# One change at six places of an encoder kernel: order of loads, more tiles, and where the low-rank products and the output projection stand

## The chip, the cores and the metric

The kernel runs on one core of a Trainium2 chip. Its time is the device time of one execution, in microseconds (us). Before the change the median of three runs is 2454.44 us (2453.6 to 2456.31). The engines are TensorE (PE: matmuls; PEld is its loading of the stationary operand), VectorE (DVE), ScalarE (ACT), GpSimd (POOL) and SyncE (SP). Transfers between the chip's memory and a core are issued by SP and by ACT, each in the order of its own instruction stream.

## The reference

An encoder trunk of two layers works on 1024 tokens of width 1024, in float32. Each layer normalizes, mixes tokens, adds to the residual stream, normalizes again, and runs a SwiGLU feed-forward network (FFN) of hidden width 2816 (22 blocks of 128), again added to the residual stream. Cut to the parts that matter here:

```python
for layer in range(2):
    hn = rms_norm(h, mix_norm[layer])
    if layer % 2 == 0:
        h = h + hybrid_ab_mixer(hn, ...)        # spatial gating and pooling
    else:
        y, v_first = rwkv7_time_mix(hn, ...)    # recurrence over time
        h = h + y
    hn = rms_norm(h, ffn_norm[layer])
    h = h + (silu(hn @ w_gate) * (hn @ w_up)) @ w_down
return rms_norm(h, final_norm)
```

The time mixing of layer 1 makes `r`, `k`, `v` by full products, the decay and learning rate by low-rank products (`tanh(xw @ w1) @ w2`, `(xa @ a1) @ a2`), the gate by `sigmoid(xg @ g1) @ g2`. Then a state of 64x64 per head is carried over the 1024 tokens, the result is normalized per head, multiplied by the gate and sent through `w_o`.

## The kernel before, in words

The sequence is cut into two halves of 512 tokens (`h` = 0 and 1; `HT` = 512). Activations lie transposed, as 8 blocks of 128 features by 512 tokens (`KT` = 8). To keep float32 accuracy every operand is split in a high and a low part (`whi`, `wlo`; `ahi`, `alo`: `split`, a copy on ACT and a subtraction on DVE, L157 and L158). A product of one 128x128 block of weights takes three matmuls of 128x512 (`mm3`, L399 to L401). A dense block of 128 outputs is 24 matmuls.

A plan (`push`) lists all weights in the order in which they are used. `take` splits the next weight of the plan, and issues on ACT the load of the one or two behind it, into one of three `raw` tiles; the splits go to `whl()` (three tiles each of `whi` and `wlo`, L125) unless the plan names another place. Each output is summed in a bank of PSUM. In the stages of the FFN there are five such banks (`DENSE`, L390), beside the recurrence three. `residual` (L493) adds a bank to the residual stream `H[h]` on DVE and so frees it.

Work that would leave PE idle runs beside dense work: `drive` and `beside` advance one generator by the progress of another. Final instruction order on each engine comes from a scheduler that follows priorities and a simulated timeline, so the rows of order below are what the engines really get. An engine works its own rows strictly in that order.

The six places, in order of time:

1. **Down products of layer 0, half 0** (L1876 to L1900). The hidden blocks of layer 0 were made earlier and saved in memory (`hid_d`, L743). `down_steps` (L883) takes groups of two and three hidden blocks in turn, loads each block on SP (L894) into one of the tiles `hd`, or of the tiles that an earlier stage lent (`lw`, `lh`: rows that read `ahi<-hid_d`), multiplies with the down weights (`dhi`, `dlo`) and adds to `H[0]`. The residual stream of half 0 comes back by L1890 (blocks 4 to 7; the first four blocks of the first group use the lent tiles, L914), that of half 1 by L1896.
2. **The first down groups of half 1** (L1881, L1907). Four groups of three run beside the normalization and the gate of layer 1's time mixing. `project_norm` (L1088) writes the normalized activations `hn`, then `project_gate` mixes and splits them. `ahead=False` lets a group's loads wait until it begins; `slots_of(f, 4, 3)` gives four weight tiles and three activation tiles.
3. **The second product of the gate** (`project`, L1207 to L1214): eight outputs, each copied by ACT (L1212) into one of four tiles (two names, two tiles each) and stored on SP.
4. **The recurrence** (`recur`, L1440 on). `load(c)` (L1472) loads a chunk of 64 tokens on SP: `ar`, `bk` (the keys; one tile), `uv`, `XT`. At the first chunk the norm weights `lnw` (L1620) follow, and `post` loads the gate chunk `gch` and the value chunk `vch` (L1640, L1642). The state passes from half 0 to half 1 in an SBUF tile, `state_d`.
5. **Beside half 1's gate** (L1975). The eight output weights of half 0 and the first FFN blocks run beside the mixing of half 1; `LOWRANK_AT[1] = 8` puts the low-rank first products (48 matmuls with splits) after the eighth output weight, `GATE_AT[1] = 8` the gate's (48) behind them. `norm_a`, the norm of half 0 ahead of the FFN, starts there too.
6. **End of layer 1** (L2001 to L2004). The FFN of half 0 goes on with blocks 18 and 19, then half 1's output projection, then its norm, then blocks 20 and 21 of half 0 and the whole FFN of half 1. In `ffn` with `early`, gate and up products run ahead of the down product of an earlier group as `ffn_events` lists them.

Of the kernel before, what the change touches and what calls it, by code (L numbers as in the profile page):

```python
# [28 lines left out]
LOWRANK_AT, GATE_AT, MIX_AT = (2, 8), (3, 8), (1, 2)  # L29
# [14 lines left out]
def tile_trunk(  # L44
# [309 lines left out]
    push_ffn(1, 0, G1A[2], push_act(("y", 1), y_d[1]))  # L354
    for e in push_o(1):
        e()
    push_ffn(1, 0, G1A[3])
# [525 lines left out]
    def down_steps(h, groups, wslot, hslot, ahead=True, after=None, between=iter(()), at={}, first={}):  # L883

        held = {}
# [4 lines left out]
        def load(g):  # L890
            for f in g:
                if f not in held:
                    held[f] = hslot(f)
                    sp.dma_start(held[f].bitcast(F32), hid_d[h][:, f])  # L894
# [5 lines left out]
        def steps():  # L900
            for gi, g in enumerate(groups):
                load(g)
                wd = {f: take(("d", 0, h, f)) for f in g}
                if gi in at:
                    at[gi]()
                if ahead and gi + 1 < len(groups):
                    load(groups[gi + 1])
# [25 lines left out]
    def ffn(l, h, hn, fp, groups=GROUPS, last=False, nd=3, after=None, between=iter(()), early=False):  # L933
# [3 lines left out]
        for kind, f in ffn_events(groups, early):  # L937
# [25 lines left out]
            elif kind == "t":  # L963
                wd[f] = take(("d", l, h, f))
            else:
                for ff in f:
                    if not early:
                        wd[ff] = take(("d", l, h, ff))
                if last and f == groups[-1]:
                    yield from final_down(h, f, wd, hid, turned)  # L970
                    continue
                for m in range(KT):
                    o = mmt()
                    ms = slice(m * P, (m + 1) * P)
                    for i, ff in enumerate(f):
                        mm3(o, wd[ff][0][:, ms], wd[ff][1][:, ms], *hid[ff], i == 0, i == len(f) - 1)
                    residual(m, h, o)
                    if after is not None and f == groups[-1]:
                        after(m)
                    yield len(f) / 8  # L980

# [202 lines left out]
    def project(h, hn1, kp, ring, keep, before_v):  # L1184
# [21 lines left out]
        for m in range(KT):  # L1206
# [4 lines left out]
            t = tmp(("epx", "k")[m % 2], 2)  # L1211
# [225 lines left out]
    state_d = const.tile([P, 8, 64], F32, name="state_d")  # L1437
    pool.memset(state_d, 0.0)

    def recur(h, wp, stream):  # L1440
# [12 lines left out]
        C, ypair, loaded = {}, {}, [None]  # L1453
        S, Q, last = [state_d], {}, []
# [18 lines left out]
        def load(c):  # L1473
# [3 lines left out]
            sp.dma_start(bk, bk_d[h][c])  # L1477
# [83 lines left out]
        def burst(c, bkt, w1):  # L1561
# [32 lines left out]
            if cg < NCH - 1:  # L1594
                Sn = state_d if c == 7 else wt("S", 2, [P, 8, 64])
# [5 lines left out]
                S[0] = Sn  # L1601
                yield 0.1
# [8 lines left out]
            if more:  # L1611
# [5 lines left out]
                if c == 0:  # L1617
                    with tc.issue_after(loaded[0].ins):
# [79 lines left out]
        load(0)  # L1698
        with tc.issue_after(loaded[0].ins):
# [170 lines left out]
    for e in (wp_es, f_es, xt_es, actp_es, ps_es):  # L1870
# [8 lines left out]
    wslot, hslot = slots_of(f, 4, 3)  # L1879
    odd = {g: i % 2 for i, gs in enumerate(D0A) for g in gs}  # L1880
    prime_b, steps_b = down_steps(1, D0B[0], wslot, hslot, False, lambda m: sp.dma_start(h_d[1, 0][:, m, :], H[1][:, m, :]))  # L1881
    acc, add = running_sums(0)
    prime_a, steps_a = down_steps(
        0, D0A, lambda f: (lw, wslot)[odd[f]](f), lambda f: (lh, hslot)[odd[f]](f), after=add, at={len(D0A) - 1: prime_b}, first=first,
# [4 lines left out]
    for k in range(4, KT, 2):  # L1889
        a_loaded = sp.dma_start(H[0][:, k : k + 2, :], hm_d[0][:, k : k + 2, :])  # L1890

    def wa1():
        yield 2.0
        for k in range(0, KT, 2):
            with tc.issue_after(a_loaded.ins):
# [105 lines left out]
    drive(ffn(1, 0, hnA, f, G1A[2], between=take_act(("y", 1)), early=True))  # L2001
    exhaust(out_proj(1, ys))
    hnB = norm_split(1, C_FFN + 8, b)
    drive(ffn(1, 0, hnA, f, G1A[3], last=True, early=True))  # L2004
# [33 lines left out]
```

## Time and profile before

| | value |
|---|---|
| runs, median (lowest to highest) | 2454.44 us (2453.6 to 2456.31) |
| span of the profiled execution | 2450.8 us, 3.6 us under that median |
| PE busy | 97% of the span, 15567 matmuls |
| DVE busy | 60% |
| ACT busy | 38% |
| POOL busy | 9% |
| PE's longest wait | 9.7 us, for `hd<-hid_d` |
| memory traffic | 342.17 MB, mean 140 GB/s |

A row of the waits names the engine that waits, the tile that it writes and the line, then what released it: another engine or a transfer (DMA) with its tile and line, and the total, the number and the longest of these waits. A timeline's row has its start and length in us from the start of the span. In brackets stands the idle time of the engine before it, and what ended that. SPq and ACTq rows are issues of transfers; the transfer itself lands later. Matmul rows overlap: a row's 0.39 us is its length from entry to exit, while the distance from one start to the next is what each one costs. The column PEclk is the clock granted to TensorE, 1.00 being full.

### The profile page before, as it was taken

How to read it: one execution, taken by the hardware profiler on the slowest of the kernel's cores; microseconds unless marked ns; L12 is line 12 of the kernel's file. 1: busy time of each engine (PE TensorE's matmuls, PEld its weight loads, DVE VectorE, ACT ScalarE, POOL GpSimd, SP SyncE). 2: the span in 40 equal slices, each digit the busy share in tenths (PEclk: the TensorE clock that was granted, in tenths of full speed). 3: DMA queues.
4: the chain of work that ended last, by engine and by line, in shares of the span. 5: the costliest groups of instructions: out<-in, count | busy, mean ns of one | idle time of the engine just before them, and what ended most of it. 6: DMA issues, size and time to landing. Idle time of an engine off the chain costs nothing. (4 is left out here: it accounts for less than half of the span.)

```text
span 2450.8 us, 38190 instructions
## 1 busy us (share of the span) xinstructions
PE 2369.0 (97%) x15567; PEld 1945.9 (79%) x15567; DVE 1476.8 (60%) x2328; ACT 935.9 (38%) x1403; POOL 217.1 (9%) x246
## 2 busy tenths in 40 slices
PE   8999999999899999999999999999999999999998
PEld 6888888888687788778777678777888788888887
DVE  6445766655558758856767947856664446434443
ACT  6233444443114644422335744433232324322223
POOL 0200000000000033101100133201100001000001
PEclk9999999999999999999999999999999999999999
DMA  5114443334655554774435465675433422433231
GB/s 177 52 60 140 153 146 103 113 103 155 252 203 204 165 149 131 226 212 132 129 126 155 160 166 141 186 223 158 143 112 122 129 78 90 150 105 95 86 103 52
DMA packets 406767, 342.17 MB, mean 140 GB/s; under 512 B 78080, under 2 KB 351616, under 8 KB 405824
## 3 DMA queue, kind: packets, MB, share of 16 engines
q10 hardware_dynamic: 266048, 195.33, 26.3%
q1 hardware_dynamic: 140544, 144.41, 18.8%
q8 instruction: 122, 2.00, 0.3%
q14 instruction: 53, 0.43, 0.0%
HBM read 263.07 MB, written 76.61 MB: 139 GB/s over the span
## 5 line engine op out<-in xcount | busy, mean ns | idle before, releaser
L399 PE MATMUL mm<-ahi,whi 128*128 128x512 f32 x1376 | 541.0, 394 | 5.8 <-DVE h L493 3.7
L400 PE MATMUL mm<-alo,whi 128*128 128x512 f32 x1376 | 541.5, 394 | 1.1 <-DVE alo L158 1.1
L401 PE MATMUL mm<-ahi,wlo 128*128 128x512 f32 x1376 | 540.1, 393 | 1.4 <-DVE wlo L158 1.4
L157 ACT ACTIVATE whi<-raw 128x1024 fp32r<-128x1024 f32 (+1 forms) x280 | 282.0, 1013 | 557.4 <-PE mm L400 428.6
L158 DVE TENSOR_TENSOR wlo<-raw,whi 128x1024 fp32r<-128x1024 f32 (+1 forms) x280 | 328.4, 1177 | 246.5 <-ACT whi L157 231.0
L399 PEld LDWEIGHTS mm<-ahi,whi 128*128 128x128 f32 x1376 | 259.0, 188 | 63.1 <-ACT whi L157 6.2
L401 PEld LDWEIGHTS mm<-ahi,wlo 128*128 128x128 f32 x1376 | 259.2, 188 | 58.4 <-DVE wlo L158 2.7
L400 PEld LDWEIGHTS mm<-alo,whi 128*128 128x128 f32 x1376 | 259.3, 188 | 57.7 <-issue 2.5
L493 DVE TENSOR_TENSOR h<-h,mm 128x512 f32<-128x512 f32 x276 | 185.5, 684 | 162.5 <-PE mm L401 161.6
L399 PE MATMUL mm<-hidhi,wdhi 128*128 128x512 f32 x304 | 117.5, 395 | 2.9 <-ACT hidhi L958 2.3
L400 PE MATMUL mm<-hidlo,wdhi 128*128 128x512 f32 x304 | 119.7, 394 | 0.0
L401 PE MATMUL mm<-hidhi,wdlo 128*128 128x512 f32 x304 | 119.0, 391 | 0.0
L730 PE MATMUL mm<-ahi,whi 128*128 128x512 f32 x296 | 115.6, 390 | 0.0
L731 PE MATMUL mm<-alo,whi 128*128 128x512 f32 x296 | 115.2, 389 | 0.0
L732 PE MATMUL mm<-ahi,wlo 128*128 128x512 f32 x296 | 113.6, 389 | 0.0
L157 ACT ACTIVATE wdhi<-raw 128x1024 fp32r<-128x1024 f32 x42 | 43.5, 1058 | 168.0 <-PE mm L400 133.1
L955 DVE TENSOR_TENSOR sg<-sg,mm 128x512 f32<-128x512 f32 x52 | 35.7, 687 | 118.9 <-PE mm L401 118.7
L399 PE MATMUL mm<-hd,dhi 128*128 128x512 f32 x192 | 75.8, 396 | 13.8 <-DMA hd<-hid_d 10.8
L400 PE MATMUL mm<-hd,dhi 128*128 128x512 f32 x192 | 75.9, 395 | 0.0
L401 PE MATMUL mm<-hd,dlo 128*128 128x512 f32 x192 | 74.8, 393 | 0.0
L399 PEld LDWEIGHTS mm<-hidhi,wdhi 128*128 128x128 f32 x304 | 57.3, 189 | 16.0 <-ACT hidhi L958 2.7
L401 PEld LDWEIGHTS mm<-hidhi,wdlo 128*128 128x128 f32 x304 | 57.5, 189 | 11.9
(395 smaller groups left out, 4278.2 us busy)
## 6 DMA issues: line engine op xcount, KB each, us to landing
raw<-in_ffn_w_down_dram ACTq DMA_DIRECT2D x88, 512.0 KB
raw<-in_ffn_w_gate_dram ACTq DMA_DIRECT2D x74, 512.0 KB
raw<-in_ffn_w_up_dram ACTq DMA_DIRECT2D x74, 512.0 KB
hid_d<-hid SPq DMA_DIRECT2D x36, 512.0 KB
hd<-hid_d SPq DMA_DIRECT2D x26, 512.0 KB
raw<-in_ab_w_in_dram ACTq DMA_DIRECT2D x16, 512.0 KB
raw<-in_ab_w_out_dram ACTq DMA_DIRECT2D x16, 512.0 KB
raw<-in_rwkv_w_r_dram ACTq DMA_DIRECT2D x16, 512.0 KB
```

What stands on the lines that cost most here:

```text
L157: act.activation(hi, src, AF.Copy)
L158: (eng or dve).tensor_tensor(out=lo, in0=src, in1=hi.bitcast(F32), op=ALU.subtract)
L399: pe.matmul(o, whi, xhi, start=first, stop=False)
L400: pe.matmul(o, whi, xlo, start=False, stop=False)
L401: pe.matmul(o, wlo, xhi, start=False, stop=last)
L493: dve.tensor_tensor(out=H[h][:, m, :], in0=H[h][:, m, :], in1=o, op=ALU.add)
L730: pe.matmul(o, wh[:, k, :], x[0][:, k, :], start=st, stop=False, skip_group_check=True)
L731: pe.matmul(o, wh[:, k, :], x[1][:, k, :], start=False, stop=False, skip_group_check=True)
L732: pe.matmul(o, wl[:, k, :], x[0][:, k, :], start=False, stop=k == 3, skip_group_check=True)
L955: dve.tensor_tensor(out=s, in0=s, in1=o, op=ALU.mult)
```

## The change

All edits keep what is computed.

- Place 1: the loads of the second group's activations come first; then `H[0]`'s blocks 4 to 7, which now wait in SP's order behind the last load of activations issued so far (`rest_a`, called when the first group starts); then the next groups' loads and `H[1]` in turn.
- Place 2: four activation tiles, not three; the next group's loads are issued one group ahead; the third weight of each group goes to the tiles of `whl()` that the side weights use, so that the four weight tiles hold two weights of two groups. In `down_steps` the next group's load now also stands ahead of the call `at[gi]`.
- Place 3: the copies use four names with two tiles each, eight in all.
- Place 4: `lnw` waits for the issue of the keys of chunk 2 as well, and `gch` and `vch` stand behind `lnw` as before. The state is stored to memory after half 0 and loaded at half 1.
- Place 5: the low-rank first products and their weights stand two output weights earlier.
- Place 6: blocks 18 to 21 are one call of `ffn`. The gate of block 20 now runs before the down product of 18 and 19; the output projection and the norm of half 1 are called after that down product (`then`). The plan of weights follows.

SP's transfers at place 1, before (tile written, tile read, size, count; `hid_d_77` is half 0, `hid_d_78` half 1, `hm_d` the saved residual streams):

```order
L743 DMA hid_d_77<-hid 128x1024
L743 DMA hid_d_78<-hid 128x1024
L1890 DMA h<-hm_d_75 128x1024 x2
L1896 DMA h<-hm_d_76 128x1024 x4
L894 DMA hd<-hid_d_77 128x1024 x3
L894 DMA ahi<-hid_d_77 128x1024
L894 DMA alo<-hid_d_77 128x1024
```

The same place in the changed kernel:

```order
L747 DMA hid_d_77<-hid 128x1024
L747 DMA hid_d_78<-hid 128x1024
L898 DMA hd<-hid_d_77 128x1024 x3
L1900 DMA h<-hm_d_75 128x1024 x2
L898 DMA hd<-hid_d_77 128x1024
L898 DMA ahi<-hid_d_77 128x1024
L898 DMA alo<-hid_d_77 128x1024
L1913 DMA h<-hm_d_76 128x1024 x2
L898 DMA hd<-hid_d_77 128x1024 x2
L1913 DMA h<-hm_d_76 128x1024 x2
```

The three activation loads moved ahead of all six loads of the residual streams, and half 1's stream moved behind the third group's activations.

DVE at place 2, before, from the norm's last step over the eight scalings to the second group's residuals (`hn_5521` is the normalized tile):

```order
L443 TENSOR_TENSOR ndg<-ident,nrs 128x512
L493 TENSOR_TENSOR h<-h,mm 128x512 x3
L158 TENSOR_TENSOR dlo<-raw,dhi 128x1024
L1088 SCALAR_TENSOR_TENSOR hn_5521<-h,vec,aux 128x512 x8
L493 TENSOR_TENSOR h<-h,mm 128x512
L158 TENSOR_TENSOR dlo<-raw,dhi 128x1024 x2
L158 TENSOR_TENSOR alo<-hn_5521,ahi 128x513
L1171 SCALAR_TENSOR_TENSOR mix<-hn_5521,vec,mix 128x512
L158 TENSOR_TENSOR alo<-hn_5521,ahi 128x513
L1171 SCALAR_TENSOR_TENSOR mix<-hn_5521,vec,mix 128x512
L158 TENSOR_TENSOR alo<-hn_5521,ahi 128x513 x6
L493 TENSOR_TENSOR h<-h,mm 128x512 x3
```

In the changed kernel:

```order
L447 TENSOR_TENSOR ndg<-ident,nrs 128x512
L497 TENSOR_TENSOR h<-h,mm 128x512 x2
L158 TENSOR_TENSOR dlo<-raw,dhi 128x1024
L497 TENSOR_TENSOR h<-h,mm 128x512
L158 TENSOR_TENSOR dlo<-raw,dhi 128x1024
L158 TENSOR_TENSOR wlo<-raw,whi 128x1024
L1094 SCALAR_TENSOR_TENSOR hn_5520<-h,vec,aux 128x512 x8
L158 TENSOR_TENSOR alo<-hn_5520,ahi 128x513 x2
L1177 SCALAR_TENSOR_TENSOR mix<-hn_5520,vec,mix 128x512 x2
L497 TENSOR_TENSOR h<-h,mm 128x512
L158 TENSOR_TENSOR alo<-hn_5520,ahi 128x513
L497 TENSOR_TENSOR h<-h,mm 128x512
```

The second group's weights are now split ahead of the eight scalings, no residual of the first group is left behind them, and the second group's residuals alternate with the splits of the activations.

SP at place 4, half 0, before:

```order
L1475 DMA ar<-ar_d_1974 128x1024
L1490 DMA XT<-xi_d_1984 32x8x32
L1620 DMA lnw<-in_rwkv_ln_w_dram 64x8x64 x2
L1640 DMA gch<-g_d_1982 128x8x128
L1642 DMA vch<-v_d_1978 64x2x512 x2
L1480 DMA uv<-v_d_1978 64x512
L1481 DMA uv<-v_d_1978 64x512
L1477 DMA bk<-bk_d_1976 128x1024
```

In the changed kernel:

```order
L1482 DMA ar<-ar_d_1974 128x1024
L1497 DMA XT<-xi_d_1984 32x8x32
L1487 DMA uv<-v_d_1978 64x512
L1488 DMA uv<-v_d_1978 64x512
L1484 DMA bk<-bk_d_1976 128x1024
L1629 DMA lnw<-in_rwkv_ln_w_dram 64x8x64 x2
L1649 DMA gch<-g_d_1982 128x8x128
L1651 DMA vch<-v_d_1978 64x2x512 x2
```

The keys of chunk 2 and the two loads ahead of them passed the five loads for the output norm.

The diff, cut:

```diff
...
 RATIO, AHEAD, INV, FINE = 3.0, 450, 5, 1
-LOWRANK_AT, GATE_AT, MIX_AT = (2, 8), (3, 8), (1, 2)
+LOWRANK_AT, GATE_AT, MIX_AT = (2, 6), (3, 8), (1, 2)
...
     push_ffn(1, 0, G1A[1])
-    push_ffn(1, 0, G1A[2], push_act(("y", 1), y_d[1]))
-    for e in push_o(1):
-        e()
-    push_ffn(1, 0, G1A[3])
+    y1, o1 = push_act(("y", 1), y_d[1]), push_o(1)
+    for i, e in enumerate(e for e in ffn_events(G1A[2] + G1A[3], True) if e[0] != "d"):
+        if e == ("u", G1A[3][0][0]):
+            for go in o1:
+                go()
+        push_ffn_event(1, 0, *e)
+        if e[0] in "gu":
+            next(y1, None)
     push_ffn(1, 1)
...
-    def down_steps(h, groups, wslot, hslot, ahead=True, after=None, between=iter(()), at={}, first={}):
-
-        held = {}
+    def down_steps(h, groups, wslot, hslot, ahead=True, after=None, between=iter(()), at={}, first={}, loaded=None):
+
+        held, loaded = {}, [] if loaded is None else loaded
         for g in groups:
...
                     held[f] = hslot(f)
-                    sp.dma_start(held[f].bitcast(F32), hid_d[h][:, f])
+                    loaded.append(sp.dma_start(held[f].bitcast(F32), hid_d[h][:, f]).ins)
...
                 wd = {f: take(("d", 0, h, f)) for f in g}
+                if ahead and gi + 1 < len(groups):
+                    load(groups[gi + 1])
                 if gi in at:
                     at[gi]()
-                if ahead and gi + 1 < len(groups):
-                    load(groups[gi + 1])
                 for m in range(KT):
...
-    def ffn(l, h, hn, fp, groups=GROUPS, last=False, nd=3, after=None, between=iter(()), early=False):
+    def ffn(l, h, hn, fp, groups=GROUPS, last=False, nd=3, after=None, between=iter(()), early=False, then={}):
         dests["d"] = lambda: (fp.tile([P, D], F32R, tag="wdhi", bufs=nd, name="wdhi"),
...
                     yield len(f) / 8
+                if f[-1] in then:
+                    then[f[-1]]()
...
             pe.matmul(o, g2b[:96, ms], keep["gst"][:96], start=False, stop=True)
-            t = tmp(("epx", "k")[m % 2], 2)
+            t = tmp(("k", "epx", "av", "sg")[m % 4], 2)
             act.activation(t, o, AF.Copy)
...
             )
-    state_d = const.tile([P, 8, 64], F32, name="state_d")
-    pool.memset(state_d, 0.0)
+    state_d = dram.tile([P, 8, 64], F32, name="state_d")
...
         lnw = wt("lnw", 1, [P, 8, 64])
-        C, ypair, loaded = {}, {}, [None]
-        S, Q, last = [state_d], {}, []
+        C, ypair, loaded, keys = {}, {}, [None], [None]
+        S, Q, last = [wt("S", 2, [P, 8, 64])], {}, []
+        if h == 0:
+            pool.memset(S[0], 0.0)
...
             bk = wt("bk", 1, [P, 8, 2, 64])
-            sp.dma_start(bk, bk_d[h][c])
+            keys[0] = sp.dma_start(bk, bk_d[h][c])
             uv = wt("uv", 2, [P, 2, 8, 64])
...
             if cg < NCH - 1:
-                Sn = state_d if c == 7 else wt("S", 2, [P, 8, 64])
+                Sn = wt("S", 2, [P, 8, 64])
                 os_ = smt()
...
                 S[0] = Sn
+                if c == 7:
+                    sp.dma_start(state_d, Sn)
                 yield 0.1
...
                 if c == 0:
-                    with tc.issue_after(loaded[0].ins):
+                    with tc.issue_after(loaded[0].ins), tc.issue_after(keys[0].ins):
                         for r in range(2):
...
         load(0)
+        if h:
+            sp.dma_start(S[0], state_d)
         with tc.issue_after(loaded[0].ins):
...
     ha_pool, ha_es = open_pool(name="ha0", bufs=1, side="left")
-    wslot, hslot = slots_of(f, 4, 3)
+    wslot, hslot = slots_of(f, 4, 4)
     odd = {g: i % 2 for i, gs in enumerate(D0A) for g in gs}
-    prime_b, steps_b = down_steps(1, D0B[0], wslot, hslot, False, lambda m: sp.dma_start(h_d[1, 0][:, m, :], H[1][:, m, :]))
+    third = {g[2] for g in D0B[0]}
+    prime_b, steps_b = down_steps(1, D0B[0], lambda f: whl() if f in third else wslot(f), hslot, True, lambda m: sp.dma_start(h_d[1, 0][:, m, :], H[1][:, m, :]))
     acc, add = running_sums(0)
+    hid_loads = []
+
+    def rest_a():
+        for k in range(4, KT, 2):
+            with tc.issue_after(hid_loads[-1]):
+                sp.dma_start(H[0][:, k : k + 2, :], hm_d[0][:, k : k + 2, :])
+
     prime_a, steps_a = down_steps(
-        0, D0A, lambda f: (lw, wslot)[odd[f]](f), lambda f: (lh, hslot)[odd[f]](f), after=add, at={len(D0A) - 1: prime_b}, first=first,
+        0, D0A, lambda f: (lw, wslot)[odd[f]](f), lambda f: (lh, hslot)[odd[f]](f), after=add, at={0: rest_a, len(D0A) - 1: prime_b}, first=first, loaded=hid_loads,
     )
...
         H[h] = pl.tile([P, KT, HT], F32, tag="h", name="h")
-    for k in range(4, KT, 2):
-        a_loaded = sp.dma_start(H[0][:, k : k + 2, :], hm_d[0][:, k : k + 2, :])
...
         for k in range(0, KT, 2):
-            with tc.issue_after(a_loaded.ins):
+            with tc.issue_after(hid_loads[-1]):
                 sp.dma_start(H[1][:, k : k + 2, :], hm_d[1][:, k : k + 2, :])
...
     ys = open_act(("y", 1), b)
-    drive(ffn(1, 0, hnA, f, G1A[2], between=take_act(("y", 1)), early=True))
-    exhaust(out_proj(1, ys))
-    hnB = norm_split(1, C_FFN + 8, b)
-    drive(ffn(1, 0, hnA, f, G1A[3], last=True, early=True))
+    hnB = []
+
+    def out_b():
+        exhaust(out_proj(1, ys))
+        hnB.extend(norm_split(1, C_FFN + 8, b))
+
+    drive(ffn(1, 0, hnA, f, G1A[2] + G1A[3], last=True, between=take_act(("y", 1)), early=True, then={G1A[2][0][-1]: out_b}))
     drive(ffn(1, 1, hnB, f, last=True, early=True))
...
```

## The prediction

> **What bounds the kernel now.** I read the page first, then the waits of TensorE, then the timelines of the engines around each wait. The page's span and busy rows:
>
> ```profile
> span 2450.8 us, 38190 instructions
> ...
> PE 2369.0 (97%) x15567; PEld 1945.9 (79%) x15567; DVE 1476.8 (60%) x2328; ACT 935.9 (38%) x1403; POOL 217.1 (9%) x246
> ```
>
> TensorE (PE) sets the end: it idles 2450.8 - 2369.0 = 82 us in all, and no edit here takes away a matmul. So a gain can only come out of those 82 us and out of stretches in which PE runs on a lower clock. The view of who waited for whom on PE (total us, times, longest) names the waits that this change can reach:
>
> ```profile
> PE mm L399 <- DMA hd<-hid_d: 10.8, 2, 9.7
> PE mm L399 <- DVE h L493: 8.7, 7, 2.5
> ...
> PE sm L1460 <- DMA bk<-bk_d: 4.2, 2, 2.2
> ...
> PE mm L399 <- ACT hidhi L958: 2.5, 2, 2.3
> ```
>
> The reader sees one large wait for a transfer, and a handful of waits of 1 to 2.5 us. They lie in different stages, so each is priced at its own place and the prices are added.
>
> **Place 1, the first down groups of half 0.** Timelines of SP's queue and of PE (start, length, what; in brackets the idle time before and its releaser), then two stretches (length, PE busy and matmuls, loads, DVE, ACT, POOL, granted clock, DMA share, GB/s), the second an undisturbed one:
>
> ```profile
> 612.99 6.16 SPq L743 DMA_DIRECT2D hid_d<-hid  x3
> 621.48 0.80 SPq L1890 DMA_DIRECT2D h<-hm_d  x2
> 622.36 2.14 SPq L1896 DMA_DIRECT2D h<-hm_d  x4
> 624.55 2.53 SPq L894 DMA_DIRECT2D hd<-hid_d  x3
> ```
>
> ```profile
> 636.50 0.77 PE L399 MATMUL mm<-hd,dhi 128*128 128x512 f32 x1 [9.71 <-DMA hd<-hid_d]
> ```
>
> ```profile
> 636.50:640.50 4.00, 4.00 (x10) 3.19 (x11) 2.32 (x2) 1.06 (x1) 0.00 (x0) 0.51 1.02 408
> ...
> 2000.00:2050.00 50.00, 50.00 (x226) 41.57 (x225) 23.17 (x27) 16.10 (x20) 0.09 (x1) 1.00 0.35 106
> ```
>
> At full clock a matmul takes 50/226 = 0.221 us. PE waits 9.71 us for the second group's activations, because six loads of the residual streams are ahead of them (each load 128x1024 numbers of four bytes, 0.52 MB). Then it issues 10 matmuls in 4.0 us at clock 0.51, where 18 would fit: 8 x 0.221 = 1.8 us. Together 11.5 us. The change issues the group's three loads first, straight after the last save, about 2.3 us before 621.48. Three of these at the 408 GB/s of that row take 3.9 us, so by estimate they are there at about 624 to 626, before PE asks at 626.8. What is late next is the residual of half 0, which those loads are now ahead of. VectorE's row shows when it was first added:
>
> ```profile
> 626.21 0.68 DVE L493 TENSOR_TENSOR h<-h,mm 128x512 f32<-128x512 f32 x1
> ```
>
> From an issue at 621.48 it had landed by 626.21, that is within 4.7 us. With 3.9 us of transfers ahead, of which 2.3 go out earlier, it comes 0 to 3.9 us later. Behind it on VectorE stand seven residual additions and the splits of the next weights, and PE has only the second group's first output (9 matmuls, 2.0 us) before it needs banks that these additions free. I take 1.5 us of new wait between 0 and 4, nearer the low end since the loads merely change places, and 0.5 us (0 to 1.5) for the third group's weights, which come through the same full stretch and are now wanted some 11 us sooner. Place 1: 11.5 - 1.5 - 0.5 = 9.5 us (6 to 11.5).
>
> **Place 2, the first groups of half 1 beside the gate.** PE's three gaps, what VectorE did meanwhile, the stage as a whole, and ScalarE's splits of the side weights in it (ns shortest/median/longest):
>
> ```profile
> 766.81 0.47 PE L399 MATMUL mm<-hd,dhi 128*128 128x512 f32 x1 [1.23 <-ACT dhi L157]
> ...
> 770.92 0.47 PE L399 MATMUL mm<-hd,dhi 128*128 128x512 f32 x1 [1.12 <-DMA hd<-hid_d]
> ...
> 780.39 0.50 PE L399 MATMUL mm<-hd,dhi 128*128 128x512 f32 x1 [1.71 <-DVE h L493]
> ```
>
> ```profile
> 764.23 1.23 DVE L158 TENSOR_TENSOR dlo<-raw,dhi 128x1024 fp32r<-128x1024 f32 x1 [0.86 <-ACT dhi L157]
> 765.37 5.35 DVE L1088 SCALAR_TENSOR_TENSOR hn<-h,vec,aux 128x512 f32<-128x512 f32 x8
> ...
> 776.04 3.70 DVE L158 TENSOR_TENSOR alo<-hn,ahi 128x513 fp32r<-128x513 f32 x6
> 779.66 1.88 DVE L493 TENSOR_TENSOR h<-h,mm 128x512 f32<-128x512 f32 x3
> ```
>
> ```profile
> 760.00:852.00 92.00, 87.84 (x380) 70.01 (x379) 80.92 (x113) 59.20 (x88) 4.99 (x10) 1.00 0.51 160
> ```
>
> ```profile
> L157 ACT ACTIVATE whi<-raw x5: 828/1044/1062, 778.1 to 847.3; 128x1024 fp32r<-128x1024 f32 x4, 128x768 fp32r<-128x768 f32 x1
> ```
>
> The gaps make 1.23 + 1.12 + 1.71 = 4.06 us: weights with no free tile, then residuals that queue behind eight norm scalings (5.35 us) and six splits (3.70 us). More tiles and the next group ahead cure the first. In VectorE's new order the last residuals of the first group stand ahead of the eight scalings, and those of the second are spread among the splits: they cure the others. The eight scalings still block VectorE for 5.35 us and it is busy 80.92 of 92 us, so not all will come out: 3.0 us (0 to 4.1).
>
> **Place 3, the copies of the gate's second product.** ScalarE's copy, PE's wait for it, and the stretch after:
>
> ```profile
> 854.89 0.60 ACT L1212 ACTIVATE epx<-mm 128x512 f32<-128x512 f32 x1 [2.62 <-DMA g_d<-epx]
> ```
>
> ```profile
> 855.54 0.79 PE L399 MATMUL mm<-ghi,whi 128*128 128x512 f32 x1 [2.01 <-ACT epx L1212]
> ```
>
> ```profile
> 855.50:858.90 3.40, 3.36 (x7) 2.32 (x8) 0.00 (x0) 1.31 (x3) 0.00 (x0) 0.51 0.58 144
> ```
>
> A copy waits for the store of the copy four before it. With two tiles under each of four names, all eight copies have their own, and ScalarE (0.60 us each) outruns PE (four matmuls, 0.9 us). Worth 2.01 us, and at full clock 3.4/0.221 = 15.4 matmuls fit where 7 ran: 8.4 x 0.221 = 1.9 us. Half 1 has only small gaps there; 0.3 us. Place 3: 4.2 us (2 if the two new names are still held by their other users, to 5).
>
> Of the clock, this row shows a half-clock stretch after a gap of only 2.01 us. [...]
>
> **Place 4, loads of the recurrence.** SP's queue, and PE:
>
> ```profile
> 1090.70 2.13 SPq L1620 DMA_DIRECT2D lnw<-in_rwkv_ln_w_dram  x2
> ...
> 1094.98 0.54 SPq L1480 DMA_DIRECT2D uv<-v_d  x1
> ...
> 1096.25 0.53 SPq L1477 DMA_DIRECT2D bk<-bk_d  x1
> ```
>
> ```profile
> 1103.48 0.40 PE L1460 MATMUL sm<-ar,bk 64*64 64x128 f32 x2 [2.24 <-DMA bk<-bk_d]
> ```
>
> The keys are issued after the norm weights, the gate chunk and the value chunk. Now they go 1094.98 - 1090.70 = 4.3 us earlier, more than the 2.24 us waited; the other half's wait is the rest of the 4.2 us in the view of waits. With 0.8 us for the clock after it (0 to 1.7; few full-size matmuls run there) that is 5.0 us. The keys have one tile, so they may wait for its last reader and hold up what is queued behind them on SP, whose users come much later. The state now leaves to memory and returns at half 1, one more load ahead of the residual stream. I take off 0.5 us: 4.5 us (2 to 5.9).
>
> **Place 5, the low-rank products two weights earlier.** VectorE's part of the norm chain, and PE's later waits in that stage:
>
> ```profile
> 1349.27 0.15 DVE L440 TENSOR_SCALAR nrs<-aux 128x4 f32<-128x4 f32 x1
> ...
> 1351.46 0.69 DVE L443 TENSOR_TENSOR ndg<-ident,nrs 128x512 f32<-128x512 f32 x1 [0.90 <-POOL nrs L404]
> ```
>
> ```profile
> 1381.02 0.50 PE L399 MATMUL mm<-ahi,whi 128*128 128x512 f32 x1 [1.46 <-ACT whi L157]
> ...
> 1408.72 0.80 PE L1291 MATMUL aux<-ta,a 128*128 128x512 f32 x1 [2.47 <-DVE a L165]
> ```
>
> This one can cost. Today the 48 low-rank matmuls follow the last output weight and hide the norm, with 30 matmuls from PE's sums to the diagonal's product and 15 from there to the FFN's first matmul. Now it is 9 and none. From the sums to the end of the diagonal took 1351.46 + 0.69 - 1349.27 = 2.9 us; 9 matmuls cover 2.0. Then a split, a mix (0.7 us, as the scalings) and the first scaling and its split must pass: about 3 us uncovered. That is some 4 us of new wait. Against it, about ten VectorE operations of the mixing are done sooner, which should shorten later waits: a third of the 2.47 and of the 1.46, plus the halved clock that may follow the former (up to 3.5 us). Net -1 us (-6 to +5).
>
> **Place 6, layer 1's y activations and output weights.** PE's three gaps, the stretch after the first, and at the norm later VectorE's last split and the FFN matmul that reads it:
>
> ```profile
> 1954.61 1.65 PE L399 MATMUL mm<-hidhi,wdhi 128*128 128x512 f32 x3 [2.26 <-ACT hidhi L958]
> ...
> 1960.47 0.50 PE L399 MATMUL mm<-hidhi,wdhi 128*128 128x512 f32 x1 [0.61 <-DVE h L493]
> ...
> 1964.00 0.50 PE L399 MATMUL mm<-ahi,whi 128*128 128x512 f32 x1 [1.17 <-DVE h L493]
> ```
>
> ```profile
> 1954.60:1958.00 3.40, 3.39 (x8) 2.67 (x9) 1.71 (x3) 1.06 (x1) 0.00 (x0) 0.51 0.82 275
> ```
>
> ```profile
> 2070.82 0.69 DVE L158 TENSOR_TENSOR alo<-hn,ahi 128x512 fp32r<-128x512 f32 x1
> ```
>
> ```profile
> 2078.40 0.39 PE L399 MATMUL mm<-ahi,whi 128*128 128x512 f32 x1
> ```
>
> The down product of two groups starts as soon as the second's hidden tile is made, and finds it unfinished. Twenty-four matmuls of the next gate (5.3 us) now stand between. The gaps make 4.04 us, the clock (15.4 - 8) x 0.221 = 1.6, together 5.6. The price: the norm's cover falls from 88 to 68 matmuls, 4.4 us, of the 2078.40 - 2071.51 = 6.9 us by which the last split is early; so nothing is lost there. The residual gaps may partly recur: 4.5 us (2.5 to 5.6).
>
> **The sum.** 9.5 + 3.0 + 4.2 + 4.5 - 1.0 + 4.5 = 24.7 us off the profiled span of 2450.8, which is 2426.1. The median of the runs, 2454.44, is 3.6 us above that span, so 2429.7, say 2430 us. All bounds at their worst leave 6.5 us (2448), all at their best 37 (2417). Gaps that nothing here touches may meet or miss a halved clock as they shift, some 1.7 us each way; over several such gaps I allow 3 us.
>
> **Rivals.** (a) Half is given back: VectorE's one queue, 88% busy at place 2, becomes the wait at places 1, 2 and 5, which fall to their lower bounds, with half a us less or so at the others: 6 + 0 + 4 + 4 - 6 + 4 = 12 us, so 2442. For it: the waits of PE at 2 and 5 already end on that queue. Against: the largest term is a transfer. Chance 0.25. (b) The early weights pay: place 5 gives +5 and place 1 all of it, 33 us, 2421: 0.10. (c) The halved clock has other causes than these gaps and stays: 20.4 us, 2434: 0.04. (d) The transfers are only exchanged: at place 1 the residual's wait takes the 9.7 us over, the DMA engines being full at share 1.02 there, and (a) holds elsewhere: 2 to 4 us, 2451, no change: 0.06. (e) Slower: at place 2 the third weight of each group takes a tile from the three that the side weights share. If these then cannot be split ahead, each of the five side weights and four thirds costs a split on both engines, 1.05 + 1.23 = 2.3 us, and after such a gap 1.9 us of clock: 9 x 4.2 = 38 us against 24.7 won, 2468. It decides from six of the nine on; ScalarE is busy only 59 of 92 us there, so I think most find a tile: 0.05. My forecast, within some 8 us of 2430, has the remaining 0.50.
>
> A measurement of this kernel tells about 0.2%, 5 us, from no change. Faster than that is my forecast with (a), (b), (c), less a tail: 0.88; same 0.06; slower 0.06. The range that leaves out two in ten runs from 2418 to 2445.
>
> **What would show it.** Right: no wait over 3 us of PE for hd, and a DMA share near 1 still around 625 to 640; the g2 copy and bk waits gone from PE's list; the first hidhi wait gone. Place 5 wrong: no new wait before that FFN block, or one over 6 us. Wrong as a whole: PE idle still above 70 us, or waits for whi in the stage of place 2.

## The result, and the profile after

The changed kernel ran in 2435.37 us (median, 2434.62 to 2435.89), the kernel before beside it in 2455.38 us: a ratio of 0.9909, with a 95% interval of 0.9892 to 0.9926. That is 20.0 us off, where 24.7 us had been forecast. In a later comparison (below) the same kernel had 2438.01 us against 2456.7, a ratio of 0.9922 (0.9910 to 0.9933).

The page of the changed kernel, and PE's waits in it (what was waited for: total us, times, longest):

```profile
span 2433.5 us, 38175 instructions
...
PE 2362.3 (97%) x15567; PEld 1940.8 (80%) x15567; DVE 1478.4 (61%) x2328; ACT 935.4 (38%) x1403; POOL 218.0 (9%) x246
```

```profile
PE mm L403 <- DVE h L497: 6.6, 7, 1.2
...
PE mm L403 <- ACT whi L157: 4.9, 3, 4.0
PE sm L1469 <- DMA bk<-bk_d: 4.8, 2, 3.4
...
PE mm L403 <- ACT hidhi L962: 2.9, 2, 2.6
...
PE mm L403 <- ACT ahi L157: 2.6, 1, 2.6
```

PE's idle time fell from 82 to 71 us, and its busy time by 7 us though it does the same matmuls: fewer of them ran on the halved clock. The clock record of the trace has 58 us at the halved clock before and 40 us here. In the execution of the later comparison it has 54 us (and PE idles 67 us), so this part changes from one execution to the next. The wait for `hd` has left the list, and so has that for the keys of chunk 2 (L1460 before, L1467 now). The row that remains, L1469, is that of each half's first chunk. It grew from 2.2 us (L1462 before) to 4.8, and to 4.2 in the later execution; no run shows why. The `hidhi` wait is still there, and there are new ones of 4.0 us for `whi` and 2.6 us for `ahi`.

Place 1 in the changed kernel, on SP, DVE and PE, and the stretch as a whole (before it: PE busy 39.60 of the same 50 us, clock 0.90):

```profile
619.47 1.76 SPq L898 DMA_DIRECT2D hd<-hid_d  x3
622.00 0.80 SPq L1900 DMA_DIRECT2D h<-hm_d  x2
```

```profile
628.90 3.84 DVE L497 TENSOR_TENSOR h<-h,mm 128x512 f32<-128x512 f32 x6 [0.91 <-DMA h<-hm_d]
```

```profile
627.10 0.39 PE L403 MATMUL mm<-hd,dhi 128*128 128x512 f32 x1
...
629.65 0.50 PE L403 MATMUL mm<-hd,dhi 128*128 128x512 f32 x1 [0.34 <-DVE h L497]
```

```profile
600.00:650.00 50.00, 48.97 (x214) 39.57 (x214) 27.75 (x37) 12.40 (x15) 0.12 (x1) 1.00 0.74 272
```

The loads go out at 619.47, and PE passes into the second group at 627.10 without a wait. VectorE does wait for the residual stream, from 628.0 to 628.9, and PE for VectorE, but only 0.34 us. The DMA engines were full from 620 to 640 (share 1.01; before the change 0.91 over the same 20 us, and 1.00 to 1.03 from 625 to 640), so the transfers did not become fewer; only their order was other.

At place 4 the product that waited 2.24 us for the keys of chunk 2 now starts without a wait:

```profile
1086.80 0.38 PE L1467 MATMUL sm<-ar,bk 64*64 64x128 f32 x2
```

Where the time went, stage by stage, is told by the starts of single matmuls that occur in all kernels (us; each column runs from the mark before it): the first product with `hd`; the first `aux<-talo,a` behind the gate's copies; the first `sm<-ar,bk` of the recurrence; the sums of half 1's norm; the second and the third mark again for the second half; the end. The third row is the changed kernel in the later comparison, the rows below it are the experiments.

| kernel (one execution each) | to first hd | groups beside gate 0, copies | projection 0 | recurrence 0 to norm | beside gate 1, copies | projection 1 | recurrence 1 to end |
|---|---|---|---|---|---|---|---|
| before | 636.5 | 228.2 | 195.8 | 238.6 | 125.6 | 201.7 | 824.4 |
| changed | 627.1 | 220.0 | 198.2 | 235.5 | 123.3 | 204.1 | 825.4 |
| changed, again | 626.4 | 220.8 | 199.3 | 234.8 | 125.1 | 204.4 | 824.2 |
| 6 taken back | 627.4 | 220.7 | 197.0 | 236.0 | 123.4 | 202.7 | 819.7 |
| own tiles for u | 625.3 | 220.5 | 197.9 | 236.9 | 126.6 | 202.4 | 819.7 |
| both | 627.6 | 219.9 | 198.3 | 236.5 | 126.4 | 204.8 | 819.3 |
| 5 taken back | 626.9 | 219.8 | 200.2 | 235.1 | 127.6 | 203.2 | 831.9 |
| 1 taken back | 636.0 | 221.9 | 197.2 | 235.7 | 123.6 | 202.6 | 826.0 |
| 2 taken back | 625.9 | 222.5 | 199.3 | 239.0 | 126.1 | 203.9 | 828.0 |
| 3 taken back | 626.2 | 225.6 | 199.2 | 241.0 | 128.7 | 203.4 | 823.8 |
| 4 taken back | 625.6 | 220.0 | 200.2 | 239.3 | 124.9 | 204.5 | 827.2 |
| 4 taken back, again | 627.4 | 220.4 | 199.2 | 238.8 | 126.4 | 202.5 | 829.4 |
| 5 alone | 635.4 | 227.1 | 196.6 | 238.9 | 127.3 | 204.4 | 829.1 |
| 1 alone | 625.9 | 226.1 | 197.9 | 235.4 | 126.3 | 204.3 | 828.1 |

In the first two rows places 1 to 3 bring 9.4 + 8.2 us, place 4's first half 3.1, place 5's stage 2.3. The projections, which no edit touches, lose 2.4 us each. PE, VectorE and ScalarE have the same order in projection 0 before and after, and over the 14 executions it takes 195.8 to 200.2 us, so this is a spread between executions as far as the record shows. The execution of the kernel before that was profiled lies 3.6 us under the first median, so the table's differences add up to 17.3 and 15.7 us and not to 20.0 and 18.7. From the second recurrence on nothing is won: what place 4 gains there, place 6 loses again.

### The profile page after: what moved, and what is told of

Same layout as the page of the kernel before. It is cut to its first block, busy times and chain, and to the rows that moved or that the text cites. A ratio compares the mean times of both kernels' runs of the same rounds, so it can differ in the third digit from the quotient of the medians.

```text
span 2433.5 us, 38175 instructions
## 1 busy us (share of the span) xinstructions
PE 2362.3 (97%) x15567; PEld 1940.8 (80%) x15567; DVE 1478.4 (61%) x2328; ACT 935.4 (38%) x1403; POOL 218.0 (9%) x246
## 5 line engine op out<-in xcount | busy, mean ns | idle before, releaser
L157 ACT ACTIVATE whi<-raw 128x1024 fp32r<-128x1024 f32 (+2 forms) x284 | 286.3, 1014 | 558.5 <-PE mm L404 432.5
L158 DVE TENSOR_TENSOR wlo<-raw,whi 128x1024 fp32r<-128x1024 f32 (+2 forms) x284 | 333.4, 1178 | 231.1 <-ACT whi L157 206.1
L404 PEld LDWEIGHTS mm<-alo,whi 128*128 128x128 f32 x1376 | 259.9, 189 | 57.0 <-issue 2.9
L158 DVE TENSOR_TENSOR wdlo<-raw,wdhi 128x1024 fp32r<-128x1024 f32 x42 | 51.4, 1223 | 26.3 <-ACT wdhi L157 26.2
L404 PEld LDWEIGHTS mm<-hidlo,wdhi 128*128 128x128 f32 x304 | 57.1, 188 | 12.1 <-DVE hidlo L963 0.5
L735 PEld LDWEIGHTS mm<-alo,whi 128*128 128x128 f32 x296 | 55.6, 188 | 11.8 <-issue 0.2
```

The source lines that it names most:

```text
L157: act.activation(hi, src, AF.Copy)
L158: (eng or dve).tensor_tensor(out=lo, in0=src, in1=hi.bitcast(F32), op=ALU.subtract)
L404: pe.matmul(o, whi, xlo, start=False, stop=False)
L735: pe.matmul(o, wh[:, k, :], x[1][:, k, :], start=False, stop=False, skip_group_check=True)
```

## The experiments

**Place 6 back.** The plan of weights and the four calls at the end are as before.

```diff
-    drive(ffn(1, 0, hnA, f, G1A[2] + G1A[3], last=True, ..., then={G1A[2][0][-1]: out_b}))
+    drive(ffn(1, 0, hnA, f, G1A[2], between=take_act(("y", 1)), early=True))
+    exhaust(out_proj(1, ys))
+    hnB = norm_split(1, C_FFN + 8, b)
+    drive(ffn(1, 0, hnA, f, G1A[3], last=True, early=True))
```

> The changed kernel with place 6 put back (blocks 18-19, then the output projection, then 20-21, as before). Theory: place 6 costs about 4.6 us net (the lead over the kernel before falls from 21.8 us at the end of the recurrence to 17.2 us at the end), so this runs at 2435.4 - 4.6 = 2431 us, and PE's wait of 4.0 us for whi ahead of half 1's FFN is gone. Rival: the loss comes from elsewhere in that stage (the clock, the final norm); then 2434 to 2437 us and the wait stays. My forecast on record had place 6 worth +4.5 us, which would give 2440 us here.

Measured: 2430.52 us against 2457.82, ratio 0.9893 (0.9876 to 0.9909). PE's waits from 1925 to 2090 us in the changed kernel, and in this one:

```profile
PE mm L403 <- ACT whi L157: 4.0, 1, 4.0
PE mm L403 <- ACT hidhi L962: 2.6, 1, 2.6
PE mm L403 <- DVE h L497: 2.4, 2, 1.2
```

```profile
PE mm L399 <- ACT hidhi L958: 2.6, 1, 2.6
PE mm L399 <- DVE h L493: 1.5, 2, 1.2
...
```

The last column of the table falls by 5 us and the `whi` wait is gone, as the theory said. The `hidhi` wait stays in both: place 6 never touched it.

**Own tiles for u.** Place 6 stays; the final norm's products no longer use the `raw` tiles.

```diff
-                u = wst.tile([P, D], F32, tag="raw", name="u")[:, :HT]
+                u = fin_pool.tile([P, HT], F32, tag="u", bufs=2, name="u")
```

> The changed kernel, place 6 kept; only the last norm's tile u gets two tiles of its own and no longer takes one of the three raw tiles through which the weights come. Theory: the late weight ahead of half 1's FFN is a matter of raw tiles that the four u hold until their store is done; then the 4.0 us wait and the halved clock behind it (1.7 us) go and the time is about 2430 us. Rival: ScalarE's own order (its copies and stores stand ahead of the weight's load) makes the load late; then the wait stays above 3 us and the time is 2434 to 2437 us.

Measured: 2431.44 us, ratio 0.9895 (0.9880 to 0.9909). What had happened in the changed kernel stands in ACT's and POOL's timelines:

```profile
2062.91 0.35 ACTq L121 DMA_DIRECT2D raw<-in_ffn_w_down_dram  x1
...
2064.33 0.40 ACTq L121 DMA_DIRECT2D raw<-in_ffn_w_gate_dram  x1
2064.82 0.86 ACTq L1792 DMA_DIRECT2D out_dram<-u  x1
...
2070.28 1.06 ACT L157 ACTIVATE whi<-raw 128x1024 fp32r<-128x1024 f32 x1 [2.22 <-DMA raw<-in_ffn_w_gate_dram]
```

```profile
2055.53 1.62 POOL L1783 TENSOR_TENSOR u<-turn,fgb 128x512 f32<-128x512 f32 x1 [1.87 <-DVE turn L1778]
...
2062.08 1.29 POOL L1783 TENSOR_TENSOR u<-turn,fgb 128x512 f32<-128x512 f32 x1
```

The final norm of half 0 stands ahead of the loads for half 1's FFN. The four `u` take turns with the weights in three tiles, so the first gate weight goes out only at 2064.33 and is split at 2070.28. PE stood still for 4.0 us. With place 6 back the norm stands ahead of these loads too, and shares the tiles; but place 6 has put 20 more of PE's matmuls in front of it. Counted from the start of the last column, PE begins that norm at 431.1 us with place 6 and at 425.9 with it back, and the gate weight is split at 462.2 and 457.5. PE is through with the down products at almost the same time (448.2 and 447.4), and so runs out of work before the later weight is there. With tiles of its own for `u`, the wait is gone with place 6 in force:

```profile
PE mm L403 <- ACT hidhi L962: 2.9, 1, 2.9
PE mm L403 <- DVE h L497: 1.4, 2, 1.2
```

So the shared tiles were the cause, and freeing them is enough. ScalarE's order is not kept apart from that: with the tiles free, the planner (the scheduler that writes the final order of instructions) issues the load of the same gate weight at 2032.60 us, ahead of the final norm's copies.

**Place 5 back** (`LOWRANK_AT = (2, 8)`).

```diff
-LOWRANK_AT, GATE_AT, MIX_AT = (2, 6), (3, 8), (1, 2)
+LOWRANK_AT, GATE_AT, MIX_AT = (2, 8), (3, 8), (1, 2)
```

> The changed kernel with the low-rank products back after the eighth output weight. Theory: place 5 took in a new wait of 2.6 us ahead of the FFN block, and gave back later waits and a halved clock of about 4.5 us, net +2 us; without it 2437 us. My forecast had it at -1 us net: 2434 us. Rival: the later halved clock went away by the shift alone and not by this edit; then this runs at 2431 to 2433 us.

Measured: 2448.29 us, ratio 0.9962 (0.9947 to 0.9977), 13 us more than the changed kernel and far from all three expectations. In its own stage the edit makes 3.4 us (127.6 against 124.2, the mean of the two executions of the changed kernel). PE's waits there, in this kernel and in the changed one:

```profile
PE mm L403 <- DVE h L497: 3.2, 1, 3.2
PE aux L1297 <- DVE a L165: 2.7, 1, 2.7
...
```

```profile
PE mm L403 <- ACT ahi L157: 2.6, 1, 2.6
PE mm L405 <- DVE wlo L158: 2.1, 2, 1.2
PE aux L1297 <- DVE a L165: 1.5, 1, 1.5
...
```

The new wait for `ahi` is there, and the others are shorter. But 7 us come from the second recurrence to the end (831.9 against 824.8), where nothing was edited. The planner gave PE, VectorE and ScalarE another order there (in the traces, from about 1650 to 1812 us). That order need not be all of it: PE idles 2.4 us more in this last column (21.5 us against 19.0 and 19.1), and the clock record has 22.5 us at the halved clock there against 13.0 and 10.4.

**Place 1 back** (the loads of `H[0]` ahead of the activations again).

```diff
-        0, D0A, ..., at={0: rest_a, len(D0A) - 1: prime_b}, first=first, loaded=hid_loads,
+        0, D0A, ..., at={len(D0A) - 1: prime_b}, first=first,
...
+    for k in range(4, KT, 2):
+        a_loaded = sp.dma_start(H[0][:, k : k + 2, :], hm_d[0][:, k : k + 2, :])
```

> The changed kernel with the loads of place 1 in the old order. Theory: the gain of 10.9 us there carries to the end undiminished, 2446 us, with the 9.7 us wait for hd back. Rival: part of a gain so early is absorbed by later transfers that come at their own time (the waits for bk at the start of both recurrences grew by 1.4 us each in the changed kernel); then undoing it costs only 6 to 9 us, 2441 to 2444 us.

Measured: 2446.11 us, ratio 0.9954 (0.9939 to 0.9968): 11 us more than the changed kernel, as the theory said. The wait is back:

```profile
PE mm L403 <- DMA hd<-hid_d: 9.1, 1, 9.1
...
```

**Places 2 and 3 back.** Three activation tiles, `ahead=False` and no shared weight tiles; and four copy tiles.

```diff
-    wslot, hslot = slots_of(f, 4, 4)
+    wslot, hslot = slots_of(f, 4, 3)
...
-            t = tmp(("k", "epx", "av", "sg")[m % 4], 2)
+            t = tmp(("epx", "k")[m % 2], 2)
```

> The changed kernel with place 2 put back (three activation tiles, no group ahead, no third weight in the shared tiles). Theory: the lead over the kernel before grew by 3.8 us in that stage, so undoing it costs about 4 us: 0.16% of the kernel before, 2439 us where the changed kernel has 2435.4. Rival: as with place 5, the planner then writes the second recurrence in another order, which moves the time by several us either way; the stage itself would still show 3.8 us, the total 2435 to 2447 us. My forecast had 3.0 us.

> The changed kernel with the copies of the gate's product in four tiles again. Theory: 2.8 us, as the lead grew there, 2438 us, with the wait of 2.0 us for the copy back. My forecast had 4.2 us, 2439.6 us. Rival: the planner's other order of both recurrences outweighs it; then the stage shows about 3 us and the total differs by more than 3 us from 2438.

Measured: without place 2 2444.26 us, ratio 0.9951 (0.9936 to 0.9966); without place 3 2449.62 us, 0.9961 (0.9946 to 0.9976). PE's waits from 755 to 850 us without place 2, and from 830 to 860 without place 3:

```profile
PE mm L403 <- DVE h L497: 1.5, 1, 1.5
PE mm L403 <- DMA hd<-hid_d: 1.5, 1, 1.5
PE mm L403 <- ACT ahi L157: 1.1, 1, 1.1
```

```profile
PE mm L403 <- ACT epx L1218: 2.6, 2, 1.7
PE mm L403 <- ACT k L1218: 1.3, 1, 1.3
```

The changed kernel has one wait of 1.0 us in the first stretch and one of 0.8 in the second:

```profile
PE mm L403 <- DVE h L497: 1.0, 1, 1.0
```

```profile
PE mm L403 <- ACT k L1218: 0.8, 1, 0.8
```

In the table's second stage place 2 is worth 2.1 us and place 3 5.2. Both totals lie 9 to 14 us above the changed kernel, and again a part of the rest is in the recurrences (239.0 and 241.0 against 235.2 in the first). The rival of both expectations, the planner's other order, explains this only in part. Without place 2 the first recurrence has the changed kernel's order on VectorE and ScalarE to the last row, and on PE but for a few neighbouring small products, and takes 3.8 us longer all the same. The clock record has 10.2 us at the halved clock there in both experiments, against 3.4 in both executions of the changed kernel.

**Place 4 back, twice**, the second time beside the changed kernel itself. Only SP's order differs, PE's is the same to the last matmul.

```diff
-                    with tc.issue_after(loaded[0].ins), tc.issue_after(keys[0].ins):
+                    with tc.issue_after(loaded[0].ins):
```

> The changed kernel with the norm weights and the gate and value chunks again issued ahead of the keys. Here the order on TensorE stays the same to the last matmul, so this is the clean price of place 4. Theory: the waits of 2.2 and 2.0 us for the keys of chunk 2 come back, 4 us in all: 2439 us. My forecast had 4.5 us plus what the state's way through memory costs. Rival: behind each of these waits the recurrence has another that ends at the same time (the changed kernel has new waits of 1.1 and 2.3 us soon after); then only 1 to 2 us, 2437 us.

> The changed kernel once more, unaltered, beside the next one. Taking back any one of places 1 to 5 cost 10 to 13 us, where the traces put 2.4 to 4 us on places 2 to 5. The rest is granted clock: the changed kernel's mean clock was 0.991, that of these five 0.988 to 0.989. If that is the luck of where halved stretches fall in the few executions seen, the changed kernel now comes out at a mean clock of 0.988 to 0.990 and 2438 to 2441 us (against 2455 before), 4 us below the next kernel. If it belongs to the kernels, it stays at 0.991 and 2435 us, 9 to 10 us below the next.

> Place 4 put back once more (TensorE's order unchanged), more executions beside the changed kernel on the same chip. Luck of the clock: 2440 to 2444 us, 4 us above the changed kernel. The kernels' own clock: 2443 to 2446 us at 0.989, 9 to 10 us above it. The span times the mean clock should in both cases be 4 us above that of the changed kernel.

Measured: 2443.46 us, 0.9952 (0.9938 to 0.9967), the first time. The second time 2444.10 us, 0.9943 (0.9929 to 0.9957), with the changed kernel at 2438.01. The difference is 6 us side by side. PE's wait for the keys of chunk 2 returns in both executions:

```profile
1091.22 0.40 PE L1467 MATMUL sm<-ar,bk 64*64 64x128 f32 x2 [1.97 <-DMA bk<-bk_d]
```

```profile
1091.97 0.40 PE L1467 MATMUL sm<-ar,bk 64*64 64x128 f32 x2 [3.02 <-DMA bk<-bk_d]
```

The mean of the two profiles is 3.9 us longer than the changed kernel's in the first recurrence (239.1 against 235.2) and 3.5 us from the second on (828.3 against 824.8). The changed kernel's mean clock, 0.991 in its first four executions, was 0.988 in the five of this comparison: the expected sign of luck. The span times the clock is 4.9 us apart in the second comparison (2412.7 and 2407.8). PE's idle time in these two columns is 35.0 and 34.9 us without place 4 and 31.6 and 31.9 with it, 3.2 us less. In three of the four places where the keys come late (two executions, two halves) a halved stretch of 3.41 us begins within 1.6 us of the wait. By estimate, from the 0.5 that the clock record has for it, it costs at most half its length, 1.7 us. So place 4 is worth 5 to 7 us. This is near the limit of what can be told: in six executions with place 4 in force and the changed kernel's order, the first recurrence takes 234.8 to 239.0 us. The 8 us between medians of two separate comparisons (2443.46 and 2435.37) hold some clock besides.

**Place 6 back and own tiles for u, together.**

> Place 6 put back and the last norm's u in tiles of its own: the two edits that each brought about 4.5 us, together. Theory: they cure the same wait (a weight held up by u), so together they bring no more than one: 2430 us, 0.989 to 0.990 of the kernel before. Rival: place 6 back still leaves the raw tiles short at the very end, and 2 us more are won: 2428 us.

Measured: 2430.86 us, ratio 0.9890 (0.9875 to 0.9904), no better than either alone. One wait, cured twice. So with tiles of its own for `u`, place 6 neither gains nor costs anything that can be told (2431.44 us with it, 2430.86 without). These three kernels are the fastest, about 5 us below the changed one in the table's last column, and cannot be told apart.

**Place 5 alone, and place 1 alone, on the kernel before.**

> The kernel before with place 5 alone. Theory: the edit itself is worth about 2.4 us in its own stage (18.3 us of lead before it, 20.7 us after, clock included), and the 13 us by which undoing it slowed the changed kernel come mostly from the other order that the planner then gives the second recurrence; alone on the kernel before it gives 2 us plus the luck of that order, 2448 to 2456 us where the kernel before has 2454.4. Rival: the edit is worth 13 us by itself: 2441 us. My forecast had it costing 1 us: 2455.5 us.

> The kernel before with place 1 alone. Theory: its 10.9 us are PE's own idle time and come whatever stands elsewhere, but the planner writes both recurrences anew, worth up to 5 us either way: 2444 us, 2439 to 2449, about 0.9955 of the kernel before. Rival: the gain is partly taken up by later waits, 2447 to 2450 us. My forecast had 9.5 us.

Measured: place 5 alone 2463.85 us, ratio 1.0032 (1.0020 to 1.0044), 0.3% slower; place 1 alone 2449.99 us, 0.9971 (0.9960 to 0.9982). Place 5 makes its own stage 1.7 us longer here and the last one 4.7 us. Place 1 brings the same 10.6 us to its mark and 2.1 us in the next stage. By the end 6.8 us of these 12.7 are left: 9.1 us are lost in the two projections, beside gate 1 and in the last stage, and 3.2 won in the first recurrence, with the planner's order of both recurrences changed. The clock record has 13.7 us at the halved clock in each projection, against 3.4 before. Two waits for `hd`, of up to 1.7 us, remain:

```profile
PE mm L399 <- DMA hd<-hid_d: 3.2, 2, 1.7
```

## Why the prediction was right, and where it was not

The range and the direction held, and the sum was 24.7 us for a measured 20.0 and 18.7 us. By its own terms:

- **Place 1**, 9.5 us: right. 9.4 us to the first product, 11 us by taking it back. The new wait that it allowed for the residuals, 1.5 us, was 0.34 us.
- **Place 2**, 3.0 us: right within what can be told. Its three gaps of 4.06 us became one of 1.0; 2.1 us by taking it back.
- **Place 3**, 4.2 us: right; places 2 and 3 share the stage that fell by 8.2 us, and taking 3 back costs it 5.2. All eight copies have tiles of their own, yet one of them still makes PE wait 0.8 us.
- **Place 4**, 4.5 us: right in its cause, sized somewhat low; 5 to 7 us. The waits themselves brought 3.2 us of idle time, for 4.2 priced. The term that was too small is the clock: 0.8 us behind one of the two waits, where one halved stretch in one execution and two in the other make up to 1.7 and 3.4 us.
- **Place 5**, -1 us (-6 to +5): not settled. The 3 us of uncovered norm came as written (2.6 us for `ahi`), but the later waits paid more than a third back. Its own stage gains 2.3 to 3.4 us in the changed kernel and loses 1.7 us on the kernel before. Nine executions with the same edits in this stage take 123.3 to 126.6 us, so differences of this size lie within the spread. The 13 us by which its removal slowed the kernel are mostly not its own stage's.
- **Place 6**, 4.5 us: wrong, it costs 5 us. Two steps failed. The gap of 2.26 us at 1954.61 was given to blocks 18 and 19. The down product behind it has 24 matmuls on PE, which makes it that of a single block, 17, the last of the group before; the edit doesn't reach it, and the changed kernel shows it again:

```profile
1932.85 0.96 PE L403 MATMUL mm<-hidhi,wdhi 128*128 128x512 f32 x3 [2.65 <-ACT hidhi L962]
```

  The residual gaps, which "may partly recur", are all there too: 2.4 us, for 1.8 before. And "so nothing is lost there" looked at the norm's splits alone. It was the weights behind the final norm that came late, through tiles which that norm shares: 4.0 us of new wait.

The miss of 4.7 us in the sum is smaller than that of place 6 (9.5 us), since places 4 and 5 came out better; that they did is luck as far as the sum goes. The measured terms (9.4, 2.1, 5.2, 5 to 7, -1.7 to 3.4, and -5) add up to 15 to 22 us. One sign that the prediction named for being wrong as a whole did come: PE idles 71 us, above its 70, in the first profile (67 in the later one). Place 6's new 4.0 us are enough to account for that.

Of the rivals, (a), half given back at VectorE's queue, did not happen: PE's waits for `h` fell from 8.7 to 6.6 us. (b) and (d) need place 5 at +5 us or the residual's wait at 9.7 us; neither is there. (e) did not come: the stage of place 2 shows no wait for `whi`.

Rival (c), by which the halved clock would be none of the gaps' doing, is refuted at place 3. In three of the four executions without that edit a halved stretch begins at the copies' waits, and in none of the ten with it. Its total does not refute it: 20.4 us (the sum less the 1.9, 0.8 and 1.6 us of clock at places 3, 4 and 6) is nearer to the measured 20.0 and 18.7 than the sum is, and the halved clock of the whole execution fell by 18 us in one execution of the changed kernel and by 4 in the other.

## What to carry to other kernels

A gap in a profile has to be tied to its block by counting matmuls on both sides before an edit is priced on it, and an operation that an edit delays has to be checked for the tiles that it shares with loads behind it, not only for its own chain. Where a planner writes the order, one edit taken back is not one edit: compare stages between fixed marks, give only the edited stage's difference to the edit, and hold it against the spread of that stage over executions in which it is left alone. Of the price of an idle gap, the part that lies in the clock differs between executions of one kernel (the changed kernel had 40 us at the halved clock in one and 54 in the other), so a difference of 5 us needs many of them.

## What the runs showed of the hardware that was not expected

How much of an execution runs at the halved clock (0.5 in the clock record of the trace) is not fixed by the kernel: the changed kernel had 40 us of it in one execution and 54 in the other. In the kernel before, halved stretches begin 849.30, 979.00, 1098.47 and 1313.51 us after the first matmul. These are 38, 35 and 63 times 3.4133 us apart, and each execution's stretches fit such a grid, with an offset that changes between executions (counted from the first matmul, 2.79 us in the kernel before and 0.17 us in the changed kernel). In the kernel before, the gaps of 2.01 us (place 3) and 2.26 us (place 6) lie inside one interval, but for less than 0.1 us, and are followed by a halved stretch; gaps of 2.24 us (at 1554 us) and 2.81 us (at 1072 us), which a point of the grid cuts in two, are followed by the full clock. All 14 traces bear it out. From 10 us on, every change of the granted clock lies on the grid of its execution to within 3 ns. Of the intervals at full clock, 126 hold 1.8 us or more of PE's idle time, and 124 of these are followed by a halved one; of 9410 that hold less than 1.0 us, one is; in between, 35 of 204 are. In the traces of the kernel before and of the changed kernel alone these are 17 of 18, none of 1348 and 3 of 30. This is counted, not tried by an edit.

The size of it shows in a stage that no edit touches, 900 to 1000 us, in the changed kernel, in its second execution, and in the one without place 4 (the column before the last two is the granted clock):

```profile
900.00:1000.00 100.00, 93.07 (x627) 76.75 (x626) 78.06 (x145) 45.87 (x67) 34.73 (x29) 0.98 0.62 169
```

```profile
900.00:1000.00 100.00, 95.54 (x619) 78.63 (x618) 76.70 (x140) 45.05 (x66) 34.67 (x29) 0.93 0.60 163
```

```profile
900.00:1000.00 100.00, 96.41 (x609) 78.96 (x604) 76.40 (x138) 45.04 (x66) 34.72 (x29) 0.91 0.59 159
```

Between the first and the last lie 18 matmuls in 100 us, of mixed sizes. The whole stage (projection 0 in the table) took 198.2, 199.3 and 200.2 us with 3.4, 13.7 and 17.1 us at the halved clock, so there the halved clock costs far less than half its length: PE idles less meanwhile (8.4, 5.3 and 4.7 us). Over a whole execution it makes several us: place 4 taken back had 2449.24 us at a mean clock of 0.988 and 2440.45 at 0.991. How much of the 4 to 7 us by which the recurrences differ is the planner's order and how much this clock is not shown; without place 2 the first recurrence has no other order and still differs by 3.8 us.
